# Row factors behind the second plain pair, the first gate and up by seven products, last forms spread

## The chip, the cores and the metric

The kernel runs on one core of a Trainium2 chip. The metric is the time of one execution in device microseconds (us), given as the median of several runs. The engines are named as in the profile: PE (TensorE), DVE (VectorE), ACT (ScalarE), POOL (GpSimd) and SP (SyncE), which issues most DMAs.

## The reference

One layer of a hybrid encoder takes one streaming step over 576 tokens: 512 frames of a new stream and 64 of a running one, with a cache of 512. The width is 2048, everything is float32.

```python
hn = rmsnorm(x, g_norm1)
q, k, v, gb, gc, hc = split(hn @ w_in)         # 2048 x 6144; 8 heads x 128, 1024 conv channels
q, k = rmsnorm(q, g_q), rmsnorm(k, g_k)        # per head
o_attn = stick_breaking(q, k_all, v_all)       # attention, strictly causal per frame
o_conv = gb * conv3_causal(gc * hc)
x = x + concat(rmsnorm(o_attn, g_attn_out), rmsnorm(o_conv, g_conv_out)) @ w_out
h2 = rmsnorm(x, g_norm2)
x = x + (silu(h2 @ w_gate) * (h2 @ w_up)) @ w_down     # inner width 5632
```

The outputs are y, the new k and v rows and the conv state, for both streams.

## The kernel before

**Number format.** Each float32 operand is split in two parts of a shorter format, hi (a cast on ACT, `nc.scalar.copy`) and lo (a subtraction on DVE); `split` (L221) does both. A product of two blocks is three matmuls: hi·hi, lo·hi and hi·lo. The moving side is always one half of the tokens, 288 columns (`HALVES`).

**Seven products.** Most of the work goes by a seven-product scheme for 2x2 blocks (Strassen's, in Winograd's form). A unit takes a column pair of 256 (blocks c = 0, 1) of one weight matrix against both token halves (i = 0, 1). Its products carry the numbers p = 1 to 7, each over 8 row pairs, that is 24 matmuls; the plain way takes 8 products. The weight side needs block sums (`weight_sums`: s1, a21, a11, a12), made in place on DVE. The moving side needs sums over frame blocks: t1 and t2 for p = 5 and 6, t3 and t4 for p = 7 and 4. These are made per pair j of 128-row blocks (`frame_sums`). `prepare(n, p)` splits the weights of a product four products ahead (`AHEAD`); `run(n, p)` issues the matmuls (L396) and what follows. `kept` (L419) is an ACT copy (`part`) of the accumulator `psy` out of PSUM; the next product into the same buffer waits for it. The pool ps_pj has three PSUM buffers; its tag is shared by psy, psv, pjo, ps_vec and ps_r.

**Stages**, in the order of PE:

1. Two heads' v by plain products while x arrives and is turned (`step0`, L661; `x_parts`, `x_sums` make the operands and the squares). During the second of them, at kt = 11 and 13 of 16, the row factors R1 of the first norm are made: `dg` (five diagonal blocks, L728, on DVE), a transpose of the small vectors (`turn_vectors`: ps_vec L252, copied to `vec` at L253), five products `ps_r` that show as ten passes (L734), and copies to R1.
2. The input units (`HEADS_A`) by seven products, from 79 us to about 600.
3. The output projection by plain products (L218), first the conv half with the attention of the heads beside it, then the heads' half. `after_b2` follows each 128 rows of the second half: it scales by g2, splits the result into the places `h2a` and `b22s` (the fourth block into b12h and b12l), sums the squares, and stores x2 to DRAM for two pairs at a time.
4. `wide("gate")` and `wide("up")` (L1371): columns 0 to 255 of gate and up (fp = 0) by plain products, 2 x 192 matmuls. The row scale R2 (`row_scale2`: two sums ss2, then logarithm and exponential on ACT) is made after the first half of gate, and `frame_sums` runs beside both and leaves t12 and t34 in SBUF.
5. Units gate and up for fp = 1 to 21. `finish` scales by R2, applies Silu (gate) or multiplies (up), and `put_forms` makes the seven forms of the hidden block, which `put_form` splits and stores to `hid_dram`, for the last pair by POOL's queue.
6. The down units (`DOWN`), whose moving side is loaded from `hid_dram`, and the stores of y.

**What orders the work.** PE's order is the program's. On ACT, DVE, POOL and SP a scheduler orders until the last gate and up units; from the unit NGU-1 on, the program's order holds there too (`manual_schedule`). `pipe.spawn` starts a piece of work that goes on with `yield n`, that is after n ticks; a tick is three matmuls in the unit stages. `order` is the list of (unit, p) and sets what is prepared and run when.

Of the kernel before, what the change touches and what calls it, by code (L numbers as in the profile page):

```python
# [16 lines left out]
P = 128  # L17
TP = 512
TS = 64
# [82 lines left out]
def tile_hybrid_stream_step(  # L102
# [47 lines left out]
    for w in (w_gate, w_up):  # L150
        for kk in range(2):
            specs.append((w[kk * 1024 : (kk + 1) * 1024, 0:256].rearrange("(k p) c -> p k c", p=P), 8, 256))
# [260 lines left out]
    def run(n, p_, early=False):  # L413
# [38 lines left out]
        elif p_ == 2:  # L452
            x = ps_z.tile([P, 512], F32, tag="z0", name="psx2")[:, :HALF]
            multiply(x, n, 2, True)
            add(0, 0, x, st["p1"])
# [43 lines left out]
    t12a, t34a = {}, {}  # L499

# [109 lines left out]
    with tc.manual_schedule(engines={mybir.EngineType.Activation, mybir.EngineType.DVE, mybir.EngineType.SP}):  # L610
# [100 lines left out]
        for kt in range(KD):  # L711
            if kt in (1, 4):
                split_wv(1, 2 + kt // 4)
            if kt in (0, 2, 4, 6, 8):
                x_squares(3 + kt // 2)
            if kt == 5:
                load_columns([("A", 1)])
            if kt == 9:
                nc.vector.reduce_sum(out=ssr, in_=ssx, axis=mybir.AxisListType.X)
                nc.vector.tensor_scalar(out=ssr, in0=ssr, scalar1=1.0 / D, scalar2=EPS, op0=ALU.mult, op1=ALU.add)  # L720
                nc.gpsimd.tensor_tensor(out=rst, in0=ssr, in1=nhalf, op=ALU.pow)
            if kt in (2, 5, 8, 11, 14):
                x_parts(3 + (kt - 2) // 3)
            if kt == 11:
                dg = [hl_tile("dg") for _ in range(2)]
                dg = [dg[i // 4][:, i % 4 * P : i % 4 * P + n] for i, (_, n) in enumerate(row_pieces())]
                for i, (_, n) in enumerate(row_pieces()):
                    nc.vector.tensor_scalar(out=dg[i][:n], in0=ident[:n, :n], scalar1=rst[:n, i : i + 1], scalar2=None,  # L728
                                            op0=ALU.mult)
            if kt == 13:  # L730
                turn_vectors(ps_pj.tile([P, 512], F32, tag="pj", name="ps_vec"))
                psr = [ps_pj.tile([P, 512], F32, tag="pj", name="ps_r1") for _ in range(2)]
                for i, (o, n) in enumerate(row_pieces()):
                    mm(psr[i // 4][:, o % TP : o % TP + n], oner.bitcast(F32)[:n, :], dg[i][:n], start=True, stop=True)  # L734
                nc.vector.tensor_copy(R1[:, :TP], psr[0])
                nc.vector.tensor_copy(R1[:, TP:], psr[1][:, :TS])
# [6 lines left out]
            step0(1, v1ps, kt)  # L743

# [20 lines left out]
    UW = T + 4  # L765
# [212 lines left out]
    def out_proj(frame, R, after=None):  # L978
        for c in range(D // 256):
            whi, wlo = next_weight()  # L980
            for j in range(2):
# [235 lines left out]
    b12pool = tc.alloc_tile_pool(name="b12pool", bufs=1, reuse_waits="tile", side="left")  # L1217
    b12h = b12pool.tile([P, NP, HALF], F32R, name="b12h")
    b12l = b12pool.tile([P, NP, HALF], F32R, name="b12l")
    acc2 = [b12pool.tile([P, HALF], F32, name=f"acc2_{i}") for i in range(2)]  # L1220

    def h2(kt, i):
        if i == 0:
            return h2a[kt]
        return b22s[kt // 2] if kt % 2 else (b12h[:, kt // 2, :], b12l[:, kt // 2, :])

    def after_b2(kt):
        for i, (a, b) in enumerate(HALVES):
            hi, lo = h2(kt, i)
            src = x2(kt)[:, a:b]  # L1230
            nc.scalar.activation(out=hi, in_=src, func=AF.Copy, scale=col("g2", kt))
            nc.vector.scalar_tensor_tensor(out=lo, in0=src, scalar=col("g2", kt), in1=hi.bitcast(F32),
                                           op0=ALU.mult, op1=ALU.subtract)
# [6 lines left out]
        if kt % 4 == 3:  # L1240
            m = kt // 4
            for k in (4 * m, 4 * m + 2):
                nc.sync.dma_start(out=x2_dram[k : k + 2].rearrange("k p t -> p k t"), in_=x2t[k // 2])

    out_proj(lambda k: mixa[k], Ra, after_b2)
    R2 = rpool.tile([P, T], F32, tag="R", name="R2", bufs=2)
    parts2 = []
    for i in range(2):
        sh, sl = parts("sq2")
        split(sh, sl, acc2[i])  # L1250
        parts2.append((sh, sl))

    def row_scale2():
# [11 lines left out]
    t34 = []  # L1265
# [5 lines left out]
    turn = [0]  # L1271

    def ps_tile(name):
        turn[0] += 1
        if turn[0] % 2:
            return ps_pj.tile([P, HALF], F32, tag="pj", name=name)
        return ps_z.tile([P, 512], F32, tag=f"z{turn[0] // 2 % 3}", name=name)[:, :HALF]

    def frame_sums():

        for j in range(NP):
            ev, od = x2(2 * j), x2(2 * j + 1)
            ge, go = col("g2", 2 * j), col("g2", 2 * j + 1)
            b11 = tmp.tile([P, HALF], F32, tag="ms", name="b11", bufs=1)
            b22 = tmp.tile([P, HALF], F32, tag="t", name="b22", bufs=1)
            nc.scalar.activation(out=b11, in_=ev[:, :HALF], func=AF.Copy, scale=ge)
            nc.scalar.activation(out=b22, in_=od[:, HALF:], func=AF.Copy, scale=go)
            ta = b12pool.tile([P, 2, HALF], F32, tag="ta", name="ta")
            tb = b12pool.tile([P, 2, HALF], F32, tag="tb", name="tb")
            t1, t2, t3, t4 = ta[:, 0], ta[:, 1], tb[:, 0], tb[:, 1]  # L1290
            nc.vector.scalar_tensor_tensor(out=t1, in0=ev[:, HALF:], scalar=ge, in1=b11, op0=ALU.mult, op1=ALU.subtract)
            nc.gpsimd.tensor_tensor(out=t2, in0=b22, in1=t1, op=ALU.subtract)
            nc.vector.scalar_tensor_tensor(out=t3, in0=ev[:, HALF:], scalar=ge, in1=b22, op0=ALU.mult, op1=ALU.subtract)
            nc.vector.scalar_tensor_tensor(out=t4, in0=od[:, :HALF], scalar=go, in1=t2, op0=ALU.mult, op1=ALU.subtract)
            two = t12[:, :, j] if j < NP - 1 else t12z
            split(two[:, :, 0, :], two[:, :, 1, :], ta)
            t34.append(ypool.tile([P, 2, 2, HALF], F32R, tag=f"y{j}", name=f"t34_{j}"))
            split(t34[j][:, :, 0, :], t34[j][:, :, 1, :], tb)
            yield 9

# [3 lines left out]
    spare = []  # L1304

    def put_form(fp, n, src):

        if fp == NFP - 1 and n > 3:
            t = spare.pop(0)()
        else:  # L1310
            t = tmp.tile([P, 2, HALF], F32R, tag="hl", name="form")
# [28 lines left out]

    def finish(kind, fp, c, i, ps, part=None):
# [8 lines left out]
        else:  # L1350
            nc.vector.tensor_tensor(out=s, in0=ps, in1=part, op=ALU.add)  # L1351
            nc.vector.tensor_tensor(out=s, in0=s, in1=R2[:, a:b], op=ALU.mult)
        if kind == "gate":
# [6 lines left out]
    def wide(kind, hold=None):  # L1360

        pss = {}
        for kk in range(2):
            whi, wlo = next_weight()
            for i, j in ((1, 0), (1, 1), (0, 0), (0, 1)):
                if kk == 0:
                    pss[j, i] = ps_tile("pw")
                for k in range(8):
                    xh, xl = h2(8 * kk + k, i)
                    for n, (w_, x_) in enumerate(((whi, xh), (wlo, xh), (whi, xl))):  # L1370
                        mm(pss[j, i], w_[:, k, j * P : (j + 1) * P], x_,  # L1371
                           start=(kk == 0 and k == 0 and n == 0), stop=(kk == 1 and k == 7 and n == 2))
                    pipe.tick()
                if kk == 1:
                    finish(kind, 0, j, i, pss[j, i])
            if hold and kk == 0:
                hold()


    pipe.spawn(frame_sums(), 20)  # L1380
    wanted += [(0, 0), (1, 0), (0, 1), (1, 1)] + [(n, c) for n in range(2, NGU) for c in range(2)]
    wanted += [(n, None) for n in range(NGU, NU)]
# [4 lines left out]
    b12pool.release()  # L1387
    w2pool = tc.alloc_tile_pool(name="w2pool", bufs=1, reuse_waits="tile", side="left")
    spool[0] = w2pool
    raw_tile["B"] = w2pool.tile([P, 2, 2048], F32, name="raw_b")  # L1390
    load_columns([("B", 0), ("B", 1)])
# [33 lines left out]
    def take_blocks(d):  # L1425

        if d in (0, 3):
# [17 lines left out]
    def spare_tile(name, q):  # L1445

        if name not in down:
# [141 lines left out]
```

## Time and profile before

| | us |
|---|---|
| three runs | 2424.18, 2425.60, 2425.93 |
| median | 2425.6 |
| the profiled execution | 2424.55 |
| its span | 2422.8 |
| outside the span | 1.75 |

The mean granted PE clock was 0.992 of full speed. In a timeline row the columns are: start, duration, engine, line of the kernel, operation, output and inputs, shapes and count; the bracket is the idle time of the engine before it and what ended it. Line numbers are those of the kernel before. "In us, x24" is the time from the first start to the last end of 24 instructions in a row.

### The profile page before, as it was taken

What the parts mean: (1) busy time and instruction counts of PE and PEld (TensorE: products, weight loads), DVE (VectorE), ACT (ScalarE), POOL (GpSimd) and SP (SyncE); (2) the same over time, 40 slices, a digit from 0 to 9 for tenths busy, and PEclk for the clock granted to TensorE, in tenths of its full rate; (3) what the DMA queues carried; (4) which work ended last, traced back from release to release, by engine and by line L of the source; (5) the groups of instructions that cost most, each with busy time, mean ns of one, the idle gap of its engine ahead of it and who ended that gap; (6) DMA issues with size and microseconds to landing.
All of it is one profiled execution on the core that took longest, in us unless ns stands there. A gap on an engine that the chain in (4) does not pass through costs nothing.

```text
span 2422.8 us, 43771 instructions
## 1 busy us (share of the span) xinstructions
PE 2357.9 (97%) x17609; PEld 2342.3 (97%) x17609; DVE 1938.7 (80%) x2810; ACT 1235.0 (51%) x2177; POOL 297.9 (12%) x385
## 2 busy tenths in 40 slices
PE   8899999998898999999999999999999899999998
PEld 8899999998888999999999999999999899999998
DVE  7889888796666767888888888888888777877875
ACT  7456656455676545444444444444444444444454
POOL 0111121120132221000000000000000001431211
PEclk9999999999999999999999999999999999999999
DMA  7434343445532233444444435444444935885642
GB/s 259 131 112 122 92 139 94 151 124 181 196 109 79 95 124 103 145 144 149 134 134 149 157 111 160 152 127 146 144 149 129 329 131 187 228 232 194 203 126 79
DMA packets 474899, 360.60 MB, mean 149 GB/s; under 512 B 11278, under 2 KB 460680, under 8 KB 474696
## 3 DMA queue, kind: packets, MB, share of 16 engines
q1 hardware_dynamic: 469528, 351.02, 45.3%
q0 software_dynamic: 5168, 6.79, 1.6%
q8 instruction: 138, 2.26, 0.4%
q14 instruction: 65, 0.53, 0.1%
HBM read 281.39 MB, written 76.37 MB: 148 GB/s over the span
## 4 chain that ended last, share of the span: by engine, by line
PE 84%; DVE 5%; ACT 3%; DMA 2%; issue 2%; POOL 1%; SPq 0%; DVEq 0%; ACTq 0%; POOLq 0%
PE psy L396 43%; PE psw L396 21%; PE psx L396 10%; PE pjo L218 6%; PE pw L1371 2%; DVE whl L223 1%; DVE wlo L180 1%; ACT whl L222 0%; PE pot L1494 0%; DVE c L857 0%; DVE raw_b L340 0%; DMA raw_a<-in_w_down_dram 0%; ACT ph L222 0%; DMA cK<-in_cache_k_dram 0%; DMA out_dram<-tokz 0%
## 5 line engine op out<-in xcount | busy, mean ns | idle before, releaser
L223 DVE TENSOR_TENSOR whl<-raw_a,whl 128x1024 fp32r<-128x1024 f32 (+4 forms) x376 | 425.9, 1133 | 71.7 <-ACT whl L222 70.3
L396 PE MATMUL psy<-t,whl 128*128 128x288 f32 x2916 | 438.0, 295 | 0.5 <-ACT part L419 0.5
L222 ACT CAST whl<-raw_a 128x1024 fp32r<-128x1024 f32 (+4 forms) x376 | 352.1, 937 | 138.9 <-PE psx L396 49.6
L396 PE MATMUL psy<-h_s,whl 128*128 128x288 f32 x2724 | 411.9, 295 | 6.6 <-ACT part L419 6.6
L396 PEld LDWEIGHTS psy<-t,whl 128*128 128x128 f32 x2916 | 403.0, 188 | 0.9 <-ACT part L419 0.7
L396 PEld LDWEIGHTS psy<-h_s,whl 128*128 128x128 f32 x2724 | 378.2, 189 | 7.1 <-ACT part L419 7.1
L396 PE MATMUL psw<-t,whl 128*128 128x288 f32 x2592 | 376.9, 295 | 0.0
L396 PEld LDWEIGHTS psw<-t,whl 128*128 128x128 f32 x2592 | 354.2, 188 | 0.2
L223 DVE TENSOR_TENSOR whl<-raw_b,whl 128x1024 fp32r<-128x1024 f32 (+5 forms) x230 | 249.2, 1084 | 88.9 <-ACT whl L222 87.9
L222 ACT CAST whl<-raw_b 128x1024 fp32r<-128x1024 f32 (+5 forms) x230 | 207.2, 902 | 212.9 <-PE psw L396 76.4
L419 ACT COPY part<-psy 128x288 f32<-128x288 f32 x303 | 121.1, 400 | 353.0 <-PE psy L396 349.7
L396 PE MATMUL psx<-h_s,whl 128*128 128x288 f32 x1122 | 166.3, 296 | 2.5 <-DVE gs L1351 2.5
L396 PEld LDWEIGHTS psx<-h_s,whl 128*128 128x128 f32 x1122 | 155.1, 190 | 2.7 <-issue 2.7
L396 PE MATMUL psw<-t34a,whl 128*128 128x288 f32 x1056 | 152.0, 297 | 5.1 <-DVE E-2_6443 L811 3.7
L222 ACT CAST whl<-s 128x1024 fp32r<-128x1024 f32 (+5 forms) x101 | 93.2, 923 | 118.3 <-PE psw L396 110.1
L396 PE MATMUL psy<-t12a,whl 128*128 128x288 f32 x1056 | 150.1, 295 | 3.1 <-ACT part L419 3.1
L396 PEld LDWEIGHTS psw<-t34a,whl 128*128 128x128 f32 x1056 | 144.8, 190 | 5.8 <-issue 3.9
L396 PEld LDWEIGHTS psy<-t12a,whl 128*128 128x128 f32 x1056 | 143.1, 188 | 4.0 <-ACT part L419 4.0
L218 PE MATMUL pjo<-mixc,whi 128*128 128x288 f32 x512 | 124.1, 309 | 0.0
L223 DVE TENSOR_TENSOR whl<-s,whl 128x1024 fp32r<-128x1024 f32 (+5 forms) x101 | 107.5, 1065 | 19.1 <-ACT whl L222 17.6
L1314 POOL DMA_DIRECT2D hid_dram<-form x3 | 2.4, 807 | 922.4 <-DVE form L223 922.4
L218 PE MATMUL pjo<-mixa,whi 128*128 128x288 f32 x512 | 102.1, 295 | 0.0
(607 smaller groups left out, 4144.8 us busy)
## 6 DMA issues: line engine op xcount, KB each, us to landing
hid_dram<-form SPq DMA_DIRECT2D x147, 288.0 KB, 2.3
raw_a<-in_w_gate_dram SPq DMA_DIRECT2D x23, 1024.0 KB, 6.1
raw_a<-in_w_up_dram SPq DMA_DIRECT2D x23, 1024.0 KB, 6.0
raw_a<-in_w_in_dram SPq DMA_DIRECT2D x22, 1024.0 KB, 5.6
raw_b<-in_w_in_dram SPq DMA_DIRECT2D x22, 1024.0 KB, 7.9
raw_b<-in_w_gate_dram SPq DMA_DIRECT2D x21, 1024.0 KB, 6.6
raw_b<-in_w_up_dram SPq DMA_DIRECT2D x21, 1024.0 KB, 8.2
h_s<-hid_dram SPq DMA_DIRECT2D x10, 2016.0 KB, 10.2
```

Of the source, the lines that this page charges most:

```text
L180: lo_eng.tensor_tensor(out=lo[:, a:b], in0=raw[:, a:b], in1=hi[:, a:b].bitcast(F32), op=ALU.subtract)
L218: mm(ps, w_[:, k, csl], x_[:, a:b], start=(k == 0 and n == 0), stop=(k == nk - 1 and n == 2))
L222: nc.scalar.copy(out=hi, in_=src)
L223: (lo_eng or nc.vector).tensor_tensor(out=lo, in0=src, in1=hi.bitcast(F32), op=ALU.subtract)
L396: mm(ps, whl[:, w_, j, :], x_, start=(start and j == 0 and q == 0), stop=(j == len(xs_) - 1 and q == 2), skip_group_check=True)
L419: nc.scalar.copy(out=t, in_=st["y"])
L1314: q.dma_start(out=hid_dram[fp][2 * n - 2 : 2 * n].rearrange("f p t -> p f t"), in_=t.bitcast(F32))
L1371: mm(pss[j, i], w_[:, k, j * P : (j + 1) * P], x_, start=(kk == 0 and k == 0 and n == 0), stop=(kk == 1 and k == 7 and n == 2))
```

## The change

- **Row factors.** `turn_vectors`, the five ps_r products and their copies move from kt = 13 to behind the loop over kt. `dg` is made at kt = 10 in a tile of its own, in front of the first unit's weights.
- **The first gate and up.** The plain wide products and their weights go; gate 0 and up 0 become units 0 and 1 of the list (NGU grows by two), run with `early` (p = 3 has its own accumulator psv). The order of their products is written out. `frame_sums` moves beside the heads' half of the output projection, one pair j after each two row blocks; t1 and t2 go through DRAM (`t12_dram`) and are loaded when the space of `mixa` is free (`load_t12`: two loads, then two small ones, t12z, for the last pair). The splits into b12h and b12l are gone. x2 is stored a pair at a time. `row_scale2` waits 19 ticks from the end of the output projection. The first products' weights are prepared within its last two row blocks, and their raw weights are loaded there.
- **Last forms.** For fp = 21, the forms that need the last results are made by `last_forms`: 16 ticks after the last result, then one each 5 ticks, in the usual form tiles instead of spare blocks.

```diff
-            if kt == 11:
-                dg = [hl_tile("dg") for _ in range(2)]
...
-            if kt == 13:
-                turn_vectors(ps_pj.tile([P, 512], F32, tag="pj", name="ps_vec"))
-                psr = [ps_pj.tile([P, 512], F32, tag="pj", name="ps_r1") for _ in range(2)]
...
             if kt == 10:
+                dg = lpool.tile([P, UW - 2], F32, tag="c0", name="dg")[:, :T]
+                for i, (o, n) in enumerate(row_pieces()):
+                    nc.vector.tensor_scalar(out=dg[:n, o : o + n], in0=ident[:n, :n], scalar1=rst[:n, i : i + 1],
+                                            scalar2=None, op0=ALU.mult)
                 prepare(-NA, 1)
             if kt == 15:
                 prepare(-NA, 2)
             step0(1, v1ps, kt)
+        turn_vectors(ps_pj.tile([P, 512], F32, tag="pj", name="ps_vec"))
+        psr = [ps_pj.tile([P, 512], F32, tag="pj", name="ps_r1") for _ in range(2)]
...
-    gu = [(kind, fp, 0, NP) for fp in range(1, NFP) for kind in ("gate", "up")]
+    gu = [(kind, fp, 0, NP) for fp in range(NFP) for kind in ("gate", "up")]
...
+    def frame_sums(j):
...
+        yield 4
+        nc.vector.scalar_tensor_tensor(out=t4, in0=od[:, :HALF], scalar=go, in1=t2, op0=ALU.mult, op1=ALU.subtract)
+        for q, t in enumerate((t1, t2)):
+            form = tmp.tile([P, 2, HALF], F32R, tag="hl", name="t12f")
+            split(form[:, 0], form[:, 1], t)
+            nc.sync.dma_start(out=t12_dram[q, j], in_=form.bitcast(F32))
+        yield 4
+        t34.append(ypool.tile([P, 2, 2, HALF], F32R, tag=f"y{j}", name=f"t34_{j}"))
+        for q, t in enumerate((t3, t4)):
+            split(t34[j][:, q, 0], t34[j][:, q, 1], t)
...
+        if kt % 2:
+            nc.sync.dma_start(out=x2_dram[kt - 1 : kt + 1].rearrange("k p t -> p k t"), in_=x2t[kt // 2])
+            pipe.spawn(frame_sums(kt // 2), 5)
+        if kt == KD - 2:
+            prepare(0, 1)
+            prepare(0, 2)
+            for _ in range(2):
+                one_sum(0)
...
     def row_scale2():
+        yield 19
...
+    pipe.spawn(row_scale2())
...
+    def load_t12():
+        yield 3
+        for q in (1, 0):
+            nc.sync.dma_start(out=t12[:, q].bitcast(F32), in_=t12_dram[q, : NP - 1].rearrange("j p f t -> p j f t"))
+            yield 6
+        for q in (1, 0):
+            nc.sync.dma_start(out=t12z[:, q].bitcast(F32), in_=t12_dram[q, NP - 1])
...
+    def last_forms(s10):
+        fp, h, tt = NFP - 1, hid.pop(NFP - 1), nc.vector.tensor_tensor
+        s00, s01, s11 = h[0, 0], h[0, 1], h[1, 1]
+        yield 16
+        tt(out=s01, in0=s01, in1=gates.pop((0, 1)), op=ALU.mult)
+        yield 4
+        tt(out=s10, in0=s10, in1=R2[:, :HALF], op=ALU.mult)
+        tt(out=s10, in0=s10, in1=gates.pop((1, 0)), op=ALU.mult)
+        for n, out, a, b in ((2, s10, None, None), (5, s00, s01, s00), (7, s01, s01, s11), (6, s11, s11, s00),
+                             (4, s10, s10, s11)):
+            yield 5
+            if a is not None:
+                tt(out=out, in0=a, in1=b, op=ALU.subtract)
+            put_form(fp, n, out)
...
-    wide("gate", row_scale2)
-    load_columns([("A", 0)])
-    wide("up", lambda: load_columns([("A", 1)]))
-    pipe.flush()
...
-    order = [(0, 1), (0, 2), (1, 1), (1, 2), (0, 6), (0, 7), (0, 5), (0, 3), (0, 4), (1, 6), (1, 7), (1, 5)]
-    for n in range(1, NU):
+    order = [(0, 1), (0, 2), (1, 1), (1, 2), (0, 3), (0, 6), (0, 5), (1, 3), (0, 7), (0, 4),
+             (1, 6), (1, 5), (1, 7), (2, 1), (1, 4), (2, 2), (2, 6), (2, 7), (2, 5)]
+    early = {0, 1}
+    for n in range(2, NU):
...
-    for k_ in range(AHEAD):
+    for k_ in range(2, AHEAD):
         prepare(*order[k_])
...
-        run(n, p_)
+        run(n, p_, n in early)
```

More of the change, by code (lines that the diff above doesn't have):

```diff
@@ L499, in tile_hybrid_stream_step @@
     t12a, t34a = {}, {}
+    UW = T + 4
     def a_frame(p_, j):
@@ L976, in x2, with out_proj @@
         return x2t[kt // 2][:, kt % 2, :]
-    def out_proj(frame, R, after=None):
+    def out_proj(frame, R, after=None, before=None):
         for c in range(D // 256):
             whi, wlo = next_weight()
+            if before:
+                before(c)
             for j in range(2):
@@ L1216, in tile_hybrid_stream_step @@
     b22s = [(places[2 * k], places[2 * k + 1]) for k in range(KD, KD + NP)]
[L1217 to L1225, printed above, removed]
+    w2pool = tc.alloc_tile_pool(name="w2pool", bufs=1, reuse_waits="tile", side="left")
@@ new lines, in tile_hybrid_stream_step @@
+    spool[0] = w2pool
+    raw_tile["B"] = w2pool.tile([P, 2, 2048], F32, name="raw_b")
+    w2pool.tile([P, NP, P], F32, tag="s1", name="s1_0")
+    apool = tc.alloc_tile_pool(name="apool", bufs=1, reuse_waits="tile", side="left")
+    acc2 = [apool.tile([P, HALF], F32, name=f"acc2_{i}") for i in range(2)]
+    wanted += [(0, 1), (1, 1), (0, 0), (1, 0)] + [(n, c) for n in range(2, NGU) for c in range(2)]
+    wanted += [(n, None) for n in range(NGU, NU)]
+    t12_dram = tc.dram_tile([2, NP, P, 2, HALF], F32, name="t12_dram")
@@ new lines, in tile_hybrid_stream_step @@
+    t34 = []
+    def frame_sums(j):
+        ev, od = x2(2 * j), x2(2 * j + 1)
+        ge, go = col("g2", 2 * j), col("g2", 2 * j + 1)
+        b11 = tmp.tile([P, HALF], F32, tag="ms", name="b11", bufs=1)
+        b22 = tmp.tile([P, HALF], F32, tag="t", name="b22", bufs=1)
+        nc.scalar.activation(out=b11, in_=ev[:, :HALF], func=AF.Copy, scale=ge)
+        nc.scalar.activation(out=b22, in_=od[:, HALF:], func=AF.Copy, scale=go)
+        t1, t2 = (tmp.tile([P, HALF], F32, tag="y", name="ta") for _ in range(2))
+        t3, t4 = (tmp.tile([P, HALF], F32, tag="r", name="tb") for _ in range(2))
+        nc.vector.scalar_tensor_tensor(out=t1, in0=ev[:, HALF:], scalar=ge, in1=b11, op0=ALU.mult, op1=ALU.subtract)
+        nc.gpsimd.tensor_tensor(out=t2, in0=b22, in1=t1, op=ALU.subtract)
+        nc.vector.scalar_tensor_tensor(out=t3, in0=ev[:, HALF:], scalar=ge, in1=b22, op0=ALU.mult, op1=ALU.subtract)
+        yield 4
[8 more added lines that the diff above has]
+            split(t34[j][:, q, 0], t34[j][:, q, 1], t)
@@ L1251, in tile_hybrid_stream_step @@
         parts2.append((sh, sl))
+    apool.release()
     def row_scale2():
+        yield 19
         for i, (a, b) in enumerate(HALVES):
@@ L1269, in frame_sum @@
         return t34[j][:, q, f, :] if p_ in (7, 4) else t12[:, q, j, f, :] if j < NP - 1 else t12z[:, q, f, :]
[L1271 to L1299, printed above, removed]
     gates = {}
     hid = {}
-    spare = []
     def put_form(fp, n, src):
[L1308 to L1311, printed above, removed]
+        t = tmp.tile([P, 2, HALF], F32R, tag="hl", name="form")
         split(t[:, 0], t[:, 1], src)
@@ L1425, in take_blocks @@
     def take_blocks(d):
+        if "z" not in down:
+            open_blocks()
         if d in (0, 3):
```

88 lines of the change are left out of this document (34 added, 54 removed).

## Prediction

> **What bounds the kernel now.** I read the page's busy times and its chain first, then TensorE's timeline, looking only for rows with idle time before them, and then the other engines' timelines around each such gap.
>
> ```profile
> PE 2357.9 (97%) x17609; PEld 2342.3 (97%) x17609; DVE 1938.7 (80%) x2810; ACT 1235.0 (51%) x2177; POOL 297.9 (12%) x385
> PE 84%; DVE 5%; ACT 3%; DMA 2%; issue 2%; POOL 1%; SPq 0%; DVEq 0%; ACTq 0%; POOLq 0%
> ```
>
> TensorE is busy for 97% of the span and carries 84% of the chain. So a change pays only if it removes matmuls or closes one of the few gaps. The unit rate comes from two full rows in the steady part:
>
> ```profile
> 1182.46 3.33 PE L396 MATMUL psw<-t,whl 128*128 128x288 f32 x24
> 1185.63 2.94 PE L396 MATMUL psy<-t,whl 128*128 128x288 f32 x21
> ```
>
> From start to start, 24 matmuls take 3.17 us, or 0.132 us each. Three gaps lie where the change works:
>
> ```profile
> 65.49 0.27 PE L252 MATMUL ps_vec<-ident,vecs 128*128 128x128 f32 x1
> 70.83 2.69 PE L734 MATMUL ps_r<-dg,oner 128*128 128x128 f32 x10 [5.07 <-DVE dg L728]
> 79.18 2.14 PE L396 MATMUL psy<-b,whl 128*128 128x288 f32 x15
> 980.37 4.34 PE L396 MATMUL psx<-h_s,whl 128*128 128x288 f32 x21 [2.52 <-DVE gs L1351]
> 995.12 0.66 PE L396 MATMUL psy<-h_z,whl 128*128 128x288 f32 x3 [0.49 <-ACT part L419]
> 1914.83 1.81 PE L396 MATMUL psy<-h_s,whl 128*128 128x288 f32 x6 [6.32 <-ACT part L419]
> 1917.15 1.57 PE L396 MATMUL psw<-h_s,whl 128*128 128x288 f32 x6
> 1918.95 0.98 PE L396 MATMUL psy<-h_s,whl 128*128 128x288 f32 x6
> ```
>
> The bracket is the idle time in front. A gap has an after-cost too. These are stretches of 2 us; after the five "busy (count)" columns comes the granted clock, then the DMA share and GB/s:
>
> ```profile
> 70.00:72.00 2.00, 1.17 (x5) 1.17 (x6) 1.87 (x8) 0.00 (x0) 0.28 (x3) 0.50 1.11 328
> 980.00:982.00 2.00, 1.63 (x7) 1.66 (x8) 2.00 (x3) 1.66 (x3) 0.80 (x1) 0.50 0.48 165
> ```
>
> Both gaps are followed by a clock of 0.50. The 21 matmuls after the gap of 2.52 took 4.34 us where 21 take 2.94: 1.40 us more. After 6.32, the eighteen from 1914.83 to 1918.95 took 4.12 us where 18 x 0.132 is 2.38: 1.74 more. The Trainium skill ("TensorE: Matmul & The Clock Gate", the section on how the oscillation bites) puts the limit at gaps of over about 3.4 us. The trace disagrees: 2.52 was enough.
>
> **1. Row factors moved behind the second plain pair.** One transpose (ps_vec) and ten passes (ps_r) move 36 matmuls later, that is 4.76 us, to 70.25. VectorE's order there decides the rest:
>
> ```profile
> 67.59 0.52 DVE L577 SCALAR_TENSOR_TENSOR tab<-st,g1c,tab 128x288 f32<-128x288 f32 x1 [1.44 <-POOL tab L575]
> 68.03 1.22 DVE L223 TENSOR_TENSOR whl<-raw_a,whl 128x1024 fp32r<-128x1024 f32 x1
> 69.83 0.75 DVE L223 TENSOR_TENSOR t34a<-tab,t34a 128x576 fp32r<-128x576 f32 x1
> 70.50 1.02 DVE L728 TENSOR_SCALAR dg<-ident,vecs 128x128 f32<-128x128 f32 x5
> ...
> 73.71 0.51 DVE L574 SCALAR_TENSOR_TENSOR tab<-st,g1c,b11s 128x288 f32<-128x288 f32 x1
> 74.56 1.36 DVE L895 TENSOR_TENSOR E<-E,R 128x576 f32<-128x576 f32 x1
> 76.94 0.75 DVE L895 TENSOR_TENSOR E<-E,R 128x576 f32<-128x576 f32 x1
> 78.28 1.22 DVE L223 TENSOR_TENSOR whl<-raw_a,whl 128x1024 fp32r<-128x1024 f32 x1
> ```
>
> In the changed order dg stands right behind the first row, so it is done at 69.0, before TensorE asks at 70.25: the gap of 5.07 goes. But the copy of ps_vec out of PSUM now stands behind the low part of the first unit's weights and two splits (from 69.0, 2.5 us, to 71.5) and behind all of frame pair 7 and the next weight split. That last block took 73.71 to 79.50 here, 5.79 us, with 2.11 us of E products among it; so 3.7 to 5.8, and walked in order 5.05. The copy comes at 76.6 to 76.8. The first unit's psy needs one of the three PSUM buffers that ps_vec and the two ps_r hold, so it starts at about 76.8. TensorE is done with the factors at 71.4, so a gap of 5.4 follows, in place of 5.07. Psy starts some 2.4 earlier than 79.18, but the slow clock now falls on unit matmuls instead of the plain pair's, which gives 2.2 back. Term: **-0.2** (-2 to +1). What would have been worth 7 us is a wait that has changed its place.
>
> **2. Heads' half of the output projection.** The sums and splits of 8 frame pairs move beside it, with 16 stores to t12_dram and per-pair x2 stores on SyncE's queue.
>
> ```profile
> 800.00:917.00 117.00, 115.53 (x862) 114.49 (x862) 80.53 (x147) 53.13 (x104) 30.75 (x37) 1.00 0.35 117
> ```
>
> VectorE has 36 of 117 us free. It gains three sums (0.5 each) and four low parts (0.46) for each of 8 pairs and loses a low part (0.5): 23 us. Three PSUM buffers give the evictions two products, 6.3 us, of slack. Term 0 (0 to +2).
>
> **3. gate 0 and up 0 by seven products.** 384 plain matmuls become 2 x 7 x 24 = 336: 48 x 0.132 = **-6.35**. The order of the instruction streams shows no other change in their number. The old first units' gaps go: 2.52 + 1.40 + 0.49 = **-4.4**.
>
> **4. The new first units.** Let T0 be the last output-projection matmul. ScalarE and VectorE now work in one chain in front of product (0,5), because its PSUM buffer is free only when ScalarE has copied the product before it, and that copy stands in ScalarE's order behind both halves of the row scale R2 and the first Silu:
>
> ```profile
> 930.58 0.44 ACT L268 ACTIVATE y<-ms 128x288 f32<-128x288 f32 x1
> 930.71 2.51 DVE L180 TENSOR_TENSOR wlo<-raw_a,whi 128x1024 fp32r<-128x1024 f32 x2 [0.36 <-ACT whi L179]
> 938.02 1.28 ACT L1354 ACT_TABLE_LOAD   x1
> 939.32 0.44 ACT L1354 ACTIVATE gs<-gs 128x288 f32<-128x288 f32 x1
> ```
>
> TensorE: (0,1), (0,2), (1,1) with the 4 sums inside, (1,2), (0,3), (0,6) at 3.17 each, with 0.3 of waiting at (1,2), are done at T0+20.1. ScalarE and VectorE: first sum ready 8.5, VectorE's mean 10.5; t34 splits and weight casts to 11.3; then on VectorE one weight low part, two weight sums of 1.2 each and five 0.45 steps until the second half's mean at 16.6; ScalarE: logarithm (17.1), table load (18.4), Silu, table load back (20.2), exponential, two weight casts of 1.0, a copy; the wanted copy ends at 23.2. So (0,5) waits 3.2 (0.5 to 6), plus 1.4 for the clock. The ScalarE page of the Trainium skill ("ScalarE: Activation LUTs", what a table load costs) adds a drain to every switch of function set, about 2.66 us in all. Here the next activation starts 1.30 after the load does, so I take the row; by the page the sum would be 2.7 worse. Three smaller waits remain, as in the same order of products at the start of the input units:
>
> ```profile
> 105.15 3.48 PE L396 MATMUL psv<-bod,whl 128*128 128x288 f32 x24 [0.49 <-ACT part L419]
> 112.66 3.46 PE L396 MATMUL psw<-t34a,whl 128*128 128x288 f32 x24 [0.86 <-DVE ghs L845]
> 119.78 3.46 PE L396 MATMUL psy<-t12a,whl 128*128 128x288 f32 x24 [0.49 <-ACT part L419]
> ```
>
> They sum to 1.84. In all 0.3 + 3.2 + 1.4 + 1.84 = **+6.7** (+3 to +12).
>
> The upper end is the DMA. Frame forms come back from DRAM in two loads of about 2 MB, issued at T0 and T0+2.5; the last pair's stores follow at T0+9.7, and t12z is loaded when these have landed. (0,6) wants it at T0+19.7.
>
> ```profile
> hid_dram<-form SPq DMA_DIRECT2D x147, 288.0 KB, 2.3
> raw_a<-in_w_gate_dram SPq DMA_DIRECT2D x23, 1024.0 KB, 6.1
> t<-hid_dram SPq DMA_DIRECT2D x6, 2016.0 KB, 12.3
> hid_dram<-form POOLq DMA_DIRECT2D x3, 288.0 KB, 5.8
> 1908.00:1910.00 2.00, 0.51 (x4) 0.28 (x3) 1.31 (x4) 0.51 (x1) 0.73 (x1) 1.00 1.11 401
> ```
>
> At 401 GB/s both loads are through by T0+11; store 5.8 and load 5.8 in a busy queue give T0+21.5. It is 2 us late, but inside the 3.2 that (0,5) loses anyway. I take that.
>
> **5. Last forms spread.** The gap of 6.32 was ScalarE's copy, late behind the last forms:
>
> ```profile
> 1912.65 0.46 DVE L223 TENSOR_TENSOR form<-ux,form 128x288 fp32r<-128x288 f32 x1 [0.50 <-ACT form L222]
> 1914.38 0.39 ACT L419 COPY part<-psy 128x288 f32<-128x288 f32 x1
> 1916.00:1932.00 16.00, 16.00 (x114) 16.00 (x114) 13.04 (x23) 7.99 (x16) 0.00 (x0) 0.92 0.77 275
> ```
>
> In the changed order this copy stands ahead of them: -6.32 - 1.74 = **-8.1**. But the forms now fall into the first three down units, where VectorE had 3 of 16 us free. They bring 12 VectorE instructions of 0.46 (5.5 us), so 2.5 don't fit; and each of five low parts waits 0.50 for ScalarE's cast, another 2.5. Forms 7, 6 and 4 also wait for a buffer whose store on POOL's queue takes 5.8 to land. Walked in order, psy of the second down unit waits 1.6, and two products later 3.2 for the copy behind the form casts, plus 1.4 of clock: **+6.2** (0 to +9).
>
> **Sum.** -0.2 - 6.35 - 4.4 + 6.7 - 8.1 + 6.2 = -6.15. The profiled run took 2424.55 us (span 2422.8 and 1.75 around it); its clock and time are those of the runs shown, 1.05 under their median. Forecast: **2418.4 us**. Under 0.2% of the median, 4.85 us, this kernel's time counts as no change: 2420.7 to 2430.5.
>
> **Rivals.** *The covers hold* (0.18): the copies get through and neither new wait arises; -0.2 - 6.35 - 4.4 + 3.5 - 8.1 + 2 = -13.6, so 2411, and up to 5 less if the ps_vec copy comes early too. For it: ScalarE is idle half the time. Against: order, not load, makes both waits. *Clock stays up* (0.05): with gaps of 3.2, under the skill's limit, the two after-costs of 1.4 vanish: 2415.6. *Table switch with drain* (0.05): 2421.1, 2.7 more. *The DMA queue makes it slower* (0.15): if each 2 MB load takes the 12.3 of its row and the second waits for the first, they are in at T0+24.6; the stores land at 27, the t12z loads behind a 6.1 us weight load at T0+35. (0,6) then waits 15.3 in place of the 3.2, with an after-cost of 1.74 in place of 1.40: +12.4, 2430.8. The gain is gone if t12z lands after T0+29. Against it speaks the 401 GB/s row; for it, that everything stands in one queue.
>
> **Numbers.** My case has 0.57: its own range is 2412 to 2424, with three quarters under 2420.7, so 0.43 faster and 0.14 same. With the covers and the clock, faster is 0.66. Same: 0.14, the table's 0.05 and 0.02 of the DMA's, 0.21. Slower: 0.13. The range 2407 to 2428 leaves out a fifth: the far part of the covers and most of the DMA case.
>
> **What would show it.** After: no gap before ps_r, but one of about 5 us before the first unit's psy, ended by a VectorE copy of vec; 336 matmuls between the output projection and unit 2; a gap of about 3 us before (0,5) ended by ACT part, with three table loads nearby; no gap of 6 us at the first down unit, but two of 1 to 3 within the next 20 us. A TensorE gap ended by the t12z load, or psy of the first unit starting before 74, would prove me wrong.

## The result and the profile after

| | median us | against before (95% interval) |
|---|---|---|
| before (19 runs) | 2425.35 | |
| changed (19 runs) | 2421.32 | 0.9982 (0.9975 to 0.9989) |

The change makes the kernel faster by 0.18%, that is by 4.0 us between the medians; the interval reaches from 2.7 to 6.1 us. The forecast was 2418.4, 6.15 us under the profiled run of the kernel before (2424.55). The time lies in the range; the sign is the one that was thought likelier. By the band of 0.2% set before, 2421.3 belongs to "same", which had 0.21, and not to "faster", which had 0.66.

The gaps in front of TensorE in the changed kernel, from its timeline in the three places (the bracket is the idle time in front and what ended it; L392 is the unit matmul, L415 the part copy):

```profile
70.06 1.42 PE L743 MATMUL ps_r<-dg,oner 128*128 128x128 f32 x10
76.61 3.94 PE L392 MATMUL psy<-b,whl 128*128 128x288 f32 x15 [5.12 <-DVE vec L249]
100.67 3.49 PE L392 MATMUL psy<-t12a,whl 128*128 128x288 f32 x24 [0.49 <-ACT part L415]
...
918.04 2.97 PE L392 MATMUL psy<-h_s,whl 128*128 128x288 f32 x21
930.24 4.58 PE L392 MATMUL psx<-h_s,whl 128*128 128x288 f32 x21 [1.96 <-DVE ms L263]
942.39 3.08 PE L392 MATMUL psy<-t,whl 128*128 128x288 f32 x21 [0.80 <-ACT part L415]
946.41 0.67 PE L392 MATMUL psv<-h_z,whl 128*128 128x288 f32 x3 [0.54 <-ACT part L415]
953.97 3.44 PE L392 MATMUL psw<-t,whl 128*128 128x288 f32 x24 [0.92 <-DVE gs L1384]
961.07 3.08 PE L392 MATMUL psy<-t,whl 128*128 128x288 f32 x21 [0.49 <-ACT part L415]
...
1903.69 0.95 PE L392 MATMUL psy<-h_s,whl 128*128 128x288 f32 x6
1919.48 1.07 PE L392 MATMUL psy<-h_s,whl 128*128 128x288 f32 x6 [0.96 <-ACT part L415]
1926.61 1.14 PE L392 MATMUL psy<-h_s,whl 128*128 128x288 f32 x6 [3.29 <-ACT part L415]
1928.99 1.64 PE L392 MATMUL psw<-h_s,whl 128*128 128x288 f32 x6
```

No gap stands before ps_r (row 70.06) any more; a gap of 5.12 stands before psy. The gap of 6.32 at the first down unit is gone (1903.69 runs on); 0.96 and 3.29 came in its place. The first new units wait four times within 20 us and once more.

Two rows of the engines beside it. The first is VectorE's in front of psy; the others are ScalarE's in front of (0,5):

```profile
76.17 0.28 DVE L249 COPY vec<-ps_vec 128x128 f32<-128x128 f32 x1
```

```profile
936.36 1.28 ACT L1393 ACT_TABLE_LOAD   x1
937.65 0.45 ACT L1393 ACTIVATE gs<-gs 128x288 f32<-128x288 f32 x1
938.12 1.28 ACT L265 ACT_TABLE_LOAD   x1
939.41 0.45 ACT L265 ACTIVATE y<-y 128x288 f32<-128x288 f32 x1
941.65 0.68 ACT L415 COPY part<-psy 128x288 f32<-128x288 f32 x2
```

**Where the time went, by stages.** Times between landmarks of the two traces, to leave out shifts between runs:

| stretch | before | after | difference | forecast |
|---|---|---|---|---|
| input, to the second gap of the input units (start taken at ps_vec) | | | -0.24 | -0.2 |
| from there to the end of the output projection | 815.48 | 817.37 | +1.89 | 0 |
| to the first down product | 989.29 | 985.65 | -3.64 | -4.05 |
| to the gap at about 2070 us | 166.60 | 165.00 | -1.60 | -1.9 |

For the first row, ps_vec now comes 4.76 us later by its own move; it started at 65.49 and 69.96, so the changed trace is 0.29 early, and 100.67 + 0.29 - 101.20 is -0.24. The second row is not the change: all of its 1.89 us lie ahead of the heads' half of the output projection, where nothing is edited; from the last gap in front of that half (816.66 and 818.02) to its end both kernels take 100.02. In the nine other kernels with the new first units behind it the whole stretch took 814.5 to 814.9 (six of them) or 817.6 to 818.0 (three). The changed kernel's profiled run waited there 8.1 us for a cache load that took 5.85 in the kernel before and 4.7 to 6.9 in the others; what sets it is not shown. The last 350 us differ by 0.7.

### The profile page after: what moved, and what is told of

The parts are those of the page before. It is cut to its first block, busy times and chain, and to the rows that moved or that the text cites. A ratio compares the mean times of both kernels' runs of the same rounds, so it can differ in the third digit from the quotient of the medians.

```text
span 2419.6 us, 43816 instructions
## 1 busy us (share of the span) xinstructions
PE 2351.4 (97%) x17561; PEld 2335.1 (97%) x17561; DVE 1958.3 (81%) x2840; ACT 1244.6 (51%) x2199; POOL 303.4 (13%) x385
## 3 DMA queue, kind: packets, MB, share of 16 engines
q8 instruction: 137, 2.24, 0.4%
## 4 chain that ended last, share of the span: by engine, by line
PE 84%; DVE 7%; ACT 4%; DMA 2%; issue 2%; POOL 1%; SPq 0%; DVEq 0%; ACTq 0%; POOLq 0%
PE psy L392 44%; PE psw L392 22%; PE psx L392 10%; PE pjo L214 4%; DVE whl L219 1%; DVE wlo L176 1%; ACT whl L218 1%; PE pj L666 1%; DVE raw_b L336 0%; PE psv L392 0%; PE pot L1493 0%; DVE c L858 0%; DMA raw_a<-in_w_down_dram 0%; DMA v_dram<-tok 0%; ACT ph L218 0%
## 5 line engine op out<-in xcount | busy, mean ns | idle before, releaser
L219 DVE TENSOR_TENSOR whl<-raw_a,whl 128x1024 fp32r<-128x1024 f32 (+4 forms) x384 | 436.8, 1138 | 69.8 <-ACT whl L218 67.8
L392 PE MATMUL psy<-t,whl 128*128 128x288 f32 x3000 | 449.4, 295 | 1.8 <-ACT part L415 1.8
L218 ACT CAST whl<-raw_a 128x1024 fp32r<-128x1024 f32 (+4 forms) x384 | 360.8, 941 | 138.0 <-PE psx L392 48.7
L392 PE MATMUL psy<-h_s,whl 128*128 128x288 f32 x2766 | 416.8, 294 | 4.9 <-ACT part L415 4.9
L392 PEld LDWEIGHTS psy<-t,whl 128*128 128x128 f32 x3000 | 414.7, 189 | 2.7 <-ACT part L415 2.5
L392 PE MATMUL psw<-t,whl 128*128 128x288 f32 x2688 | 390.5, 295 | 0.9 <-DVE gs L1384 0.9
L392 PEld LDWEIGHTS psy<-h_s,whl 128*128 128x128 f32 x2766 | 383.1, 188 | 5.6 <-ACT part L415 5.6
L392 PEld LDWEIGHTS psw<-t,whl 128*128 128x128 f32 x2688 | 366.9, 189 | 1.3 <-DVE gs L1384 1.2
L219 DVE TENSOR_TENSOR whl<-raw_b,whl 128x1024 fp32r<-128x1024 f32 (+5 forms) x234 | 252.6, 1080 | 88.3 <-ACT whl L218 87.0
L415 ACT COPY part<-psy 128x288 f32<-128x288 f32 x309 | 123.3, 399 | 354.3 <-PE psy L392 353.5
L392 PE MATMUL psx<-h_s,whl 128*128 128x288 f32 x1164 | 171.9, 296 | 2.0 <-DVE ms L263 2.0
L392 PEld LDWEIGHTS psx<-h_s,whl 128*128 128x128 f32 x1164 | 161.1, 190 | 2.2 <-DVE ms L263 2.2
L392 PE MATMUL psw<-t34a,whl 128*128 128x288 f32 x1056 | 153.2, 299 | 4.9 <-DVE E-2_6442 L812 3.5
L392 PE MATMUL psy<-t12a,whl 128*128 128x288 f32 x1056 | 150.2, 295 | 3.1 <-ACT part L415 3.1
L392 PEld LDWEIGHTS psw<-t34a,whl 128*128 128x128 f32 x1056 | 146.0, 192 | 5.6 <-issue 3.7
L392 PEld LDWEIGHTS psy<-t12a,whl 128*128 128x128 f32 x1056 | 143.2, 188 | 4.0 <-ACT part L415 4.0
```

The source lines that it names most:

```text
L218: nc.scalar.copy(out=hi, in_=src)
L219: (lo_eng or nc.vector).tensor_tensor(out=lo, in0=src, in1=hi.bitcast(F32), op=ALU.subtract)
L392: mm(ps, whl[:, w_, j, :], x_, start=(start and j == 0 and q == 0), stop=(j == len(xs_) - 1 and q == 2), skip_group_check=True)
L415: nc.scalar.copy(out=t, in_=st["y"])
```

## Experiments

All ratios are against the kernel before on the same chip, with the interval of 95%.

**The parts alone.** `r1_only` and `forms_only` add one part to the kernel before; `units_only` takes the other two out of the changed one. Edits:

```diff
  r1_only (kernel before):
-            if kt == 11:   (dg)
-            if kt == 13:   (turn_vectors, ps_r, R1)
+            if kt == 10:   (dg, then prepare(-NA, 1))
+        behind the loop:   turn_vectors, ps_r, R1
  forms_only (kernel before):
+    def last_forms(s10): ...
+            if kind == "up" and fp == NFP - 1 and (c, i) == (1, 0):
+                pipe.spawn(last_forms(s))
+                return
  units_only (changed kernel): both of these undone
```

> The kernel before with the first part of the change alone (row factors behind the second plain pair, dg at kt = 10 in a tile of its own). Theory A (a wait that changes its place: VectorE has the same work to do and the copy of ps_vec stands behind it): no gap in front of ps_r, a gap of about 5.1 us in front of the first unit's psy, which starts at about 76.6 us instead of 79.2, but with the slow clock; the input units' later products start 0.5 us earlier at most. Time 0 to 1 us under the kernel before. Rival B (the gap of 5.07 us and its after-cost are won): 5 to 7 us less.

> The kernel before with the third part of the change alone (last forms spread). Theory A: the gap of 6.3 us at the first down unit goes, gaps of about 1 and 3.3 us come in the second and third down unit, the latter with a slow clock behind it; 1 to 3 us less than before. Rival B: the forms find cover and 8 us are won. Rival C: without the other parts nothing is won, since the down units start at another state of the queues: 0.

> The changed kernel with the first and the third part undone: only gate 0 and up 0 by seven products with all that goes with it. Theory A: 48 matmuls less are 6.35 us, of which the new first units give back 2 to 3 by a wait of 2 us at (1,2), the slow clock behind it and 0.8 at (0,5): 3 to 5 us less than before. If the parts add up, r1_only, forms_only and this one give together the 4 us that the whole change gave. Rival B: the middle of the kernel (from the input units to the attention of the first head) takes 1.9 us longer in the changed kernel by a cause of the change, and this part brings it along: then 2 us less at most.

| kernel | median us | ratio |
|---|---|---|
| r1_only | 2426.22 | 1.0002 (0.9993 to 1.0011) |
| forms_only | 2422.54 | 0.9986 (0.9977 to 0.9995) |
| units_only | 2422.28 | 0.9987 (0.9978 to 0.9995) |

Their timelines' gaps, one row of r1_only, two of forms_only and three of units_only:

```profile
78.81 3.94 PE L396 MATMUL psy<-b,whl 128*128 128x288 f32 x15 [5.13 <-DVE vec L253]
```

```profile
1923.16 1.06 PE L396 MATMUL psy<-h_s,whl 128*128 128x288 f32 x6 [0.97 <-ACT part L419]
1929.72 1.06 PE L396 MATMUL psy<-h_s,whl 128*128 128x288 f32 x6 [2.72 <-ACT part L419]
```

```profile
71.54 2.69 PE L739 MATMUL ps_r<-dg,oner 128*128 128x128 f32 x10 [5.04 <-DVE dg L733]
931.91 4.59 PE L392 MATMUL psx<-h_s,whl 128*128 128x288 f32 x21 [2.24 <-DVE ms L263]
1914.25 1.81 PE L392 MATMUL psy<-h_s,whl 128*128 128x288 f32 x6 [6.30 <-ACT part L415]
```

The row factors bring nothing: the same 5 us wait stands elsewhere. Counted as in the first row of the table above, r1_only is 0.6 us later than the kernel before where the changed kernel is 0.24 earlier; neither is more than scatter. Forms and units bring about 3.4 and 3.2 us by the ratios. The three sum to some 6 us with an uncertainty of over 3, which holds the 4.4 of the whole; that they add up exactly is not shown.

**What the first unit waits for.** `vec_early` frees the PSUM buffer early; `r1_pool` also takes four subtractions from VectorE.

```diff
+            if kt == 13:
+                turn_vectors(ps_pj.tile([P, 512], F32, tag="pj", name="ps_vec"))
...
-        turn_vectors(ps_pj.tile([P, 512], F32, tag="pj", name="ps_vec"))
  r1_pool, besides, in x_parts:
+        lo_eng = nc.gpsimd if j >= NP - 2 else None
-        split(two[:, :, 0, :], two[:, :, 1, :], ta)
+        split(two[:, :, 0, :], two[:, :, 1, :], ta, lo_eng)
```

> The changed kernel with the transpose of the small vectors (ps_vec) back at kt = 13, the ps_r products staying behind the loop: the PSUM buffer that the first unit's psy waited for is free early. Theory A (VectorE is the bound there, 99% busy from 76 to 100 us): psy starts at about 71.5 us without a gap, but stops after 15 matmuls, at the transposes of the tokens, until VectorE has made E1 at about 79.5; by 100 us nothing is left, 0 to 1.5 us less than the changed kernel. Rival B (the buffer alone was the bound): 4 to 5 us less than the changed kernel.

> As vec_early, and the low parts of the frame sums of pairs 6 and 7 (four subtractions of 128x576, 0.75 us each on VectorE) on POOL. Theory A (VectorE's work is the bound from 67 to 100 us): TensorE's wait at the transposes of the tokens falls from 5.6 to about 4 us, and the products after it run 1.5 to 3 us earlier than in vec_early; 1.5 to 3 us less. Rival B (POOL's subtractions take long and hold up t2 of the last pair, for which VectorE waits): no gain or a loss.

vec_early: 2422.21, 0.9984 (0.9975 to 0.9993). r1_pool: 2422.79, 0.9988 (0.9979 to 0.9997). Neither is told apart from the changed kernel. TensorE in vec_early, then TensorE, POOL and VectorE in r1_pool:

```profile
71.88 2.25 PE L392 MATMUL psy<-b,whl 128*128 128x288 f32 x15
79.76 1.12 PE L752 MATMUL tok_a<-ident,E 128*128 128x128 f32 x4 [5.63 <-DVE E L892]
```

```profile
72.48 2.25 PE L392 MATMUL psy<-b,whl 128*128 128x288 f32 x15 [0.73 <-DVE vec L249]
81.69 1.11 PE L753 MATMUL tok_a<-ident,E 128*128 128x128 f32 x4 [6.96 <-DVE E L893]
```

```profile
67.93 1.45 POOL L219 TENSOR_TENSOR t12a<-tab,t12a 128x576 fp32r<-128x576 f32 x1 [0.79 <-ACT t12a L218]
69.33 1.42 POOL L219 TENSOR_TENSOR t34a<-tab,t34a 128x576 fp32r<-128x576 f32 x1
```

```profile
67.61 3.38 DVE L737 TENSOR_SCALAR dg<-ident,vecs 128x128 f32<-128x128 f32 x5
76.32 2.35 DVE L219 TENSOR_TENSOR whl<-raw_a,whl 128x1024 fp32r<-128x1024 f32 x1 [1.73 <-ACT whl L218]
```

In vec_early psy starts 4.7 us earlier than in the changed kernel and TensorE stops 15 matmuls later, for E1: the wait has moved again, and its size has grown by half a us. By the second gap of the input units vec_early is 1.65 us behind the changed kernel and r1_pool 2.5, counted from the start as above; vec_early was expected to be up to 1.5 ahead. The buffer alone does not hold this place; VectorE's queue is the next thing that does. But giving work to POOL failed: the five products dg take 3.38 us from 67.61 on, until POOL's two subtractions (67.93 to 70.75) are over, and a later weight split waits 1.73 for ScalarE. The wait grew to 6.96. The edit did not lighten VectorE's queue: it took out four subtractions of 0.75, 3.0 us, and dg and that weight split became 2.36 and 1.13 longer, 3.5 us (the last section tells why). So r1_pool doesn't decide whether VectorE's load or the order of the queues makes the wait, and this stays open. What would shorten the wait was not found.

**The first new units.** `psx2_z2` gives (1,2) a buffer that doesn't wait for the sums; `p7_first` also puts (0,7) ahead of (0,5).

```diff
-            x = misc("psx2") if n == 1 else ps_z.tile([P, 512], F32, tag="z0", name="psx2")
+            x = ps_z.tile([P, 512], F32, tag="z2" if n == 1 else "z0", name="psx2")
  p7_first, besides:
-    order = [(0, 1), (0, 2), (1, 1), (1, 2), (0, 3), (0, 6), (0, 5), (1, 3), (0, 7), (0, 4),
+    order = [(0, 1), (0, 2), (1, 1), (1, 2), (0, 3), (0, 6), (0, 7), (0, 5), (1, 3), (0, 4),
```

> The changed kernel with the accumulator of (1,2) in the PSUM buffer z2, free until (1,7), instead of one of the two that the sums ss2 use. Theory A (the chain of VectorE and ScalarE up to the part copy sets the place, not the buffer): no wait at (1,2), products (1,2), (0,3), (0,6) run 2 us or more earlier, and (0,5) waits 3 to 5 us for the same part copy, which still ends at about 24 us after the output projection; time within 1.5 us of the changed kernel. Rival B (the buffer was the bound): the 2 us and the slow clock behind them are won, 2 to 4 us less than the changed kernel.

> As psx2_z2, and (0,7) ahead of (0,5): (0,7) accumulates into a buffer of its own and needs no part copy, so it fills 3.17 us in front of (0,5). Theory A: (0,5) waits 0 to 1.5 us without a slow clock; 2 to 4 us less than the changed kernel. Rival B (VectorE is the bound of the whole stretch): (0,7)'s weights come late or a later product waits instead; within 1 us of the changed kernel.

psx2_z2: 2421.22, 0.9985 (0.9977 to 0.9994). p7_first: 2414.53, 0.9963 (0.9950 to 0.9975). Their gaps between the output projection and unit 2:

```profile
936.86 0.66 PE L392 MATMUL psy<-t12z,whl 128*128 128x288 f32 x3 [1.61 <-DMA t12z<-t_dram]
940.43 5.29 PE L392 MATMUL psy<-t,whl 128*128 128x288 f32 x21 [2.92 <-ACT part L415]
```

```profile
940.56 0.67 PE L392 MATMUL psy<-t12z,whl 128*128 128x288 f32 x3 [1.87 <-DMA t12z<-t_dram]
948.15 0.67 PE L392 MATMUL psv<-h_z,whl 128*128 128x288 f32 x3 [0.54 <-ACT part L415]
958.43 3.04 PE L392 MATMUL psy<-t,whl 128*128 128x288 f32 x21 [0.49 <-ACT part L415]
```

In psx2_z2 the wait at (1,2) is gone and 1.61 + 2.92 + a slow clock (5.29 for 21 matmuls instead of 2.94) stand in its place. The part copy is where the chain of VectorE and ScalarE puts it, so theory A holds. In p7_first a product that needs no part copy stands in front of it: the waits at (0,5) and (0,4) vanish and the clock stays up. And t12z comes too late in both: the load that the changed kernel's own waits still hid. From the first unit product to the first down product the traces took 985.65 us in the changed kernel, 988.08 in psx2_z2 and 981.68 in p7_first. So p7_first gains 4.0 us there, as expected; the other 2.8 of the 6.8 between the medians are not explained by it, and the five runs of p7_first reach from 2413.03 to 2418.46.

**The last forms.** `forms_ax` puts form 7 in a block of its own; `forms_10` spaces the forms by 10 ticks.

```diff
  forms_ax:
+        if fp == NFP - 1 and n == 7:
+            t = down["ax"].bitcast(F32R)
  forms_10:
-            yield 5
+            yield 10
```

> The changed kernel with form 7 of the last pair in a block of its own, so that no form's cast waits for the store of an earlier one to land. Theory A (VectorE's work and the order of ScalarE's queue make the gap of 3.3 us, the landing adds about 1): the wait of ScalarE for the store goes, the gap falls to 2 to 2.6 us; 1 to 2 us less than the changed kernel. Rival B (the landings are the whole cause): the gap falls under 1 us, 3 to 5 us less.

> The changed kernel with 10 ticks instead of 5 between the last forms. Theory A (5.5 us of VectorE's work and the buffers' landings don't fit into 25 ticks, but fit into 50): the two gaps of 1.0 and 3.3 us in the second and third down unit fall under 1 us together, nothing comes later; 3 to 5 us less than the changed kernel. Rival B (VectorE has no room in the down units at all): the gaps move to the fourth unit with the same sum. Rival C (the blocks that the later units open in the same space now wait for the forms): a new gap at down unit 4 or 5.

forms_ax: 2418.85, 0.9973 (0.9963 to 0.9983). forms_10: 2417.36, 0.9969 (0.9959 to 0.9980). ScalarE in the changed kernel, then the gap in forms_ax, then those in forms_10:

```profile
1922.97 0.43 ACT L218 CAST form<-ux 128x288 fp32r<-128x288 f32 x1 [3.02 <-DMA hid_dram<-form]
1925.83 0.43 ACT L218 CAST form<-ut 128x288 fp32r<-128x288 f32 x1 [1.91 <-DVE ut L1371]
1926.16 0.39 ACT L415 COPY part<-psy 128x288 f32<-128x288 f32 x1
```

```profile
1927.46 1.06 PE L392 MATMUL psy<-h_s,whl 128*128 128x288 f32 x6 [2.14 <-ACT part L415]
1929.17 0.97 PE L392 MATMUL psw<-h_s,whl 128*128 128x288 f32 x6
```

```profile
1931.32 1.07 PE L392 MATMUL psy<-h_s,whl 128*128 128x288 f32 x6 [0.99 <-ACT part L415]
1936.46 1.06 PE L392 MATMUL psy<-h_s,whl 128*128 128x288 f32 x6 [0.48 <-ACT part L415]
```

Without the wait for the landing the gap falls from 3.29 to 2.14: the landing was 1.15 of it. Besides, no slow clock follows (0.97 for six matmuls, where 1928.99 above shows 1.64); that this comes from the shorter gap is not shown, since none followed a gap of 3.28 in psx2_z2 either (last section). The rest is VectorE's work in too short a time, as forms_10 shows: 0.99 + 0.48 remain of 0.96 + 3.29, and nothing comes later.

**Together.** `combo` is p7_first and forms_10. `combo_z` also splits the last pair's t1 and t2 directly into t12z.

```diff
  combo_z, besides:
+            if j == NP - 1:
+                split(t12z[:, q, 0], t12z[:, q, 1], t)
+                continue
-        for q in (1, 0):
-            nc.sync.dma_start(out=t12z[:, q].bitcast(F32), in_=t12_dram[q, NP - 1])
```

> p7_first and forms_10 together. The two parts lie 970 us apart and should add up: 7 us (p7_first's first units) less some of it and 4 us (forms_10): 2410 to 2415 us, 10 to 14 less than the kernel before. If p7_first's result was scatter, 2414 to 2418.

> combo, and the last frame pair's t1 and t2 split directly into t12z, which is free by then, instead of through DRAM. Theory: the wait of 1.9 us for the load of t12z in front of (0,6)'s last matmuls goes; 0 to 2 us less than combo, since the part copy for (0,5) may be late next. Rival: the writes into the space of mixa hold up ScalarE's and VectorE's queues at the end of the output projection; no gain.

combo: 2410.66, **0.9942** (0.9930 to 0.9955), 14.7 us under the kernel before: the best version. By the traces its first units take 4.1 us less than the changed kernel's (981.51), and from the first down product to the end of the span it takes 4.4 less (511.5 for 515.9); another 2.6 lie in the unedited stretch (814.8 for 817.4). combo_z: 2415.78, 0.9966 (0.9952 to 0.9980), worse than combo. Its timeline, of TensorE and ScalarE, says why:

```profile
947.38 1.09 PE L392 MATMUL psv<-h_z,whl 128*128 128x288 f32 x3 [4.39 <-ACT part L415]
```

```profile
945.04 1.99 ACT L218 CAST whl<-raw_a 128x1024 fp32r<-128x1024 f32 x2 [2.21 <-DVE raw_a L340]
946.93 0.39 ACT L415 COPY part<-psy 128x288 f32<-128x288 f32 x1
```

The load's wait is gone, but the scheduler has ordered ScalarE otherwise, and now two weight casts that wait for VectorE's sum stand in front of the part copy for (1,3). The first units take 986.11, 4.6 more than in combo; the output projection ends no later (814.7 and 814.8 from the same gap), so the rival is not it.

## Why the prediction was right, and where not

- **Row factors, -0.2.** Right in mechanism and size: -0.24 by the traces, a ratio of 1.0002 for the part alone. The copy was forecast at 76.6 to 76.8 and came at 76.17 (76.46 without the shift of 0.29); the gap was forecast at 5.4 and measured 5.12. vec_early shows that the reason given, the PSUM buffer of ps_vec, is only the first of two waits at one place.
- **Output projection, 0.** Right: VectorE went from 67.7 of 97 us to 88.3 of 98, 20 us more (23 were forecast), and TensorE stayed without a gap:

```profile
820.00:918.00 98.00, 98.00 (x741) 98.00 (x741) 88.30 (x158) 53.97 (x111) 36.75 (x35) 1.00 0.49 168
```

- **New first units, +6.7.** The sum was right, its parts were not. Measured: 1.96 at (1,2), 1.64 of slow clock behind it (4.58 - 2.94), 0.80 at (0,5), 0.14 behind that, and 0.54 + 0.92 + 0.49: 6.5. The step that failed is the 0.3 at (1,2): VectorE was done with the mean at T0+12.2, 1.7 us later than worked out. About 1.2 of this are two low parts of squares that ran beside additions on POOL and took 1.07 and 1.06 us, where the same operation takes 0.46 in the forms (1926.29); the POOL row, then the first of the two:

```profile
921.98 1.03 POOL L1268 TENSOR_TENSOR acc<-acc,sq 128x288 f32<-128x288 f32 x1 [1.39 <-DVE whl L219]
```

```profile
922.27 1.07 DVE L219 TENSOR_TENSOR sq<-acc,sq 128x288 fp32r<-128x288 f32 x1
```

  The 3.2 at (0,5) shrank by the same delay. Its part copy ended at T0+24.3, forecast 23.2. psx2_z2 shows the two to be one wait. That the parts came to 6.5 is partly luck: vec_early, which has no edit there, waited 2.25 at (1,2) and 2.33 at (0,5), with the slow clock behind the second, in all 8.3, and took 987.43 us to the first down product.
- **Table loads.** Each took 1.28 us, and the next activation started 1.29 after (936.36 to 937.65). The drain that the Trainium skill adds ("ScalarE: Activation LUTs", what a table load costs) shows in neither of them, so the row was the right price.
- **Last forms, -8.1 + 6.2.** Right: the gaps of 1.6 and 3.2 came as 0.96 and 3.29, the clock as 1.65 (24 matmuls from 1926.61 to 1931.43 in 4.82 instead of 3.17), 5.9 for 6.2; by the landmarks, -1.6 for -1.9. The two causes named, VectorE's room and the landing, hold about 2 and 1.15 of the larger gap.
- **The clock.** 1.4 for each of two dips came as 1.64 and 1.65. (A dip is a stretch behind a gap at a granted clock of about 0.5.) The rival without dips fell for these two gaps in this trace, though not for all of their size: in psx2_z2 the same gap of the last forms, 3.28, had no dip (below). So the gap's length alone does not bring the 1.4, and the 0.05 for a trace without dips was low.
- **The DMA case** did not come: the 2 MB loads landed after 8.4 us (median of the two), not 12.3. The loads of t12z, issued from 935.27 on, landed 3.9 us later, so the first at T0+21.2, as forecast (21.5), and (0,6) came to it at T0+23.0. But t12z was nearer to being the bound than 0.15 makes one think: with the other waits gone it stops TensorE for 1.6 to 1.9 us.
- **The total.** By stages the change gives -5.5 in the two traces, forecast -6.15, and -3.6 with the unedited stretch; the median gives -4.0. The difference is about what separates single runs of this kernel, which reach from 2417.95 to 2424.97. What was misjudged is the chance of "same": with a sum of 6 and such a scatter, a result near 4.85 was as likely as not.

## What to carry to other kernels

When three engines feed one, ask of every removed wait which instruction stands next in the same queue: here one 5 us wait moved twice without shrinking. A product that needs no late copy, put in front of the one that does, was worth 4.0 us together with a free buffer; freeing the buffer that seemed to block was worth nothing by itself (0.9985 beside 0.9982). Work spread over later units needs room counted on the engine that does it: twice the spacing cost nothing and took the median from 2421.32 to 2417.36.

## What the runs showed of the hardware

Gaps of equal length cost differently. At the same product, a gap of 2.24 us in units_only was followed by 4.59 us for 21 matmuls, with a mean granted clock of 0.63; in vec_early a gap of 2.25 was followed by 3.08, at 1.00:

```profile
929.98 3.08 PE L392 MATMUL psx<-h_s,whl 128*128 128x288 f32 x21 [2.25 <-DVE ms L263]
...
942.12 4.58 PE L392 MATMUL psy<-t,whl 128*128 128x288 f32 x21 [2.33 <-ACT part L415]
```

The mean clock is the last column but two in the same two stretches, of units_only and of vec_early:

```profile
931.91:936.50 4.59, 4.59 (x23) 4.59 (x24) 4.59 (x7) 0.87 (x2) 0.00 (x0) 0.63 1.03 348
```

```profile
929.98:933.06 3.08, 3.08 (x23) 3.08 (x24) 3.08 (x5) 0.87 (x2) 0.00 (x0) 1.00 1.02 383
```

The second row of vec_early shows that its next gap, of 2.33, did dip. The gap of 1.96 in the changed kernel dipped; those of 1.87 in p7_first and 2.14 in forms_ax did not, and neither did the longer one in front of the last forms in psx2_z2, where six matmuls took 0.95 behind it:

```profile
1926.90 1.06 PE L392 MATMUL psy<-h_s,whl 128*128 128x288 f32 x6 [3.28 <-ACT part L415]
...
1928.60 0.95 PE L392 MATMUL psw<-h_s,whl 128*128 128x288 f32 x6
```

At the same place 3.29 in the changed kernel dipped, and so did 2.72 in forms_only and 3.38 to 3.41 in vec_early, p7_first and r1_pool. So between about 2 and 3.3 us the length alone doesn't tell whether the clock falls. A dip cost 1.4 to 1.7 us in most places shown here, and 2.35 in psx2_z2 (5.29 less 2.94), where two gaps stand close together. That the Trainium skill ("TensorE: Matmul & The Clock Gate", the part on the warm-up) lets the activity window run free of the kernel would explain it; no run here shows the window itself.

POOL's subtractions held VectorE up. In the changed kernel, where POOL has none, the same five products dg took a third as long as the 3.38 above:

```profile
67.74 1.02 DVE L734 TENSOR_SCALAR dg<-ident,vecs 128x128 f32<-128x128 f32 x5
```

The difference of 2.36 is most of the 2.82 that POOL's two instructions lasted. The Trainium skill ("SBUF — State Buffer", the part on the two sides of the memory) calls the port that the two engines share an exclusive lock for the whole of an instruction; these rows agree with it, as does the weight split at 76.32, with 2.35 where a split in the changed kernel takes 1.22: POOL's last subtraction ran from 76.19 to 77.59. So all that the four took from VectorE (3.0) came back as longer instructions of its own (2.36 + 1.13). The squares at 922.27, beside POOL's addition, show the same in the changed kernel.
